# S5 outputs moved from the attention stretch into the scan stretch of a hybrid encoder layer

## The chip, the cores and the metric

The kernel runs as one program on one core of a Trainium2 chip. The metric is device time in microseconds (us); lower is better. Five engines work side by side, each on its own list of instructions: TensorE (PE, matmuls and transposes), VectorE (DVE), ScalarE (ACT), GpSimd (POOL) and SyncE (SP), which issues most DMAs. PSUM, the memory that TensorE writes, is shared out here in eight buffers.

## The reference, cut to what matters

One layer: a bidirectional S5 state space model with a GLU, beside a 4-head attention into 256 memory tokens; both outputs go through one projection, a layer norm, and a mixture of 16 experts. The part in question:

```python
bu = jnp.einsum('blgc,gpc->blgp', ug, b_bar)           # inputs of the states
_, states = lax.associative_scan(_ssm_combine, (a, bu), reverse=(direction == 1), axis=1)
y = y + jnp.real(jnp.einsum('gcp,blgp->blgc', cmat, states)).reshape(bsz, L, S5_WIDTH)
...
g = jax.nn.gelu(y)
return g * jax.nn.sigmoid(g @ w_glu + b_glu)
...
kv = (mem @ w_kv).reshape(bsz, mem.shape[1], 2, MEM_HEADS, MEM_HEAD_DIM)
s = jnp.einsum('blhd,bmhd->bhlm', q, kv[:, :, 0]) * (MEM_HEAD_DIM ** -0.5)
out = jnp.einsum('bhlm,bmhd->blhd', jax.nn.softmax(s, -1), kv[:, :, 1])
```

## The kernel before

There are 2048 tokens in 16 tiles of 128, and 32 S5 groups in 8 blocks of four. The sequence is cut into 128 chunks of 16 tokens: what happens inside a chunk is a matrix product, and only one state per chunk is scanned.

The first stretch projects the tokens (`inproj_u`) and builds the S5 matrices block by block (`s5_block`); these wait in DRAM (`wid` for a block's inputs, `wod` and `kd` for its outputs).

The scan stretch treats each block in three steps. `chunk_inputs` multiplies U by the loaded `wtl` on TensorE into a PSUM buffer `pvv`, and ScalarE copies it into the state `S`, two copies a block. `scan` then copies four pieces of a rotation table `R` out of `E` (ScalarE), rotates `S` (`turn_states`: one multiply of 128x1024 on VectorE, one on GpSimd, two adds on VectorE), runs eight recurrences on VectorE, rotates back (two multiplies again, one add on VectorE and one on GpSimd), and copies the result into `SS` with eight ScalarE copies. The blocks go 6, 7, 0, 1, ... 5. `R` has two buffers; the products `m` have one, and a spare part of `S` serves every other block. In the middle stands `kv`: the keys' and values' weights in four parts, each loaded, split into two halves of 16 bits (`kvh` on ScalarE, `kvl` on VectorE) and multiplied on TensorE, and at the end eight `kh` and eight `kl` copies on ScalarE.

The attention stretch interleaves two things in a fixed TensorE order. `s5_out` takes a block's four groups; a group is eight f32 matmul passes into `py`; two groups make one `gt` copy, and after every second block four times four transposes (`trg`) with a GELU follow (`gelu`: ScalarE square, VectorE, ScalarE tanh, VectorE), written into `gT`, which lies over `S`. `attention` goes through 16 tiles in three stages (scores and exponentials; transposed probabilities two tiles later; values three tiles later); `STEPS` says how many of these stages follow each piece of `s5_out`. The blocks 0 and 1 have no attention in between and run while the scan ends; from block 2 on two stages follow each piece. `glu_weights` loads the GLU's weights over `E` once the rotations have been read, and splits them (four ScalarE, four VectorE instructions). `glu` follows.

The order on the engines other than TensorE is set by a scheduler that places instructions by its own costs and keeps each engine's list fixed from then on. TensorE's order is as written inside `manual_schedule`.

Of the kernel before, what the change touches and what calls it, by code (L numbers as in the profile page):

```python
# [9 lines left out]
F32 = mybir.dt.float32  # L10
# [3 lines left out]
ALU = mybir.AluOpType  # L14
# [39 lines left out]
STEPS = (0,) * 8 + (1,) + (2,) * 39  # L54
ATL = (2, 3)
WIP = 3
# [16 lines left out]
class Kern:  # L73
# [97 lines left out]
    def front(self, fr):  # L171
# [17 lines left out]
        with ExitStack() as s5:  # L189
            up = s5.enter_context(self.pool("up", side="left"))  # L190
            self.U = up.tile([P, 2, G, P], F32, name="U")
            att = s5.enter_context(self.pool("att", side="left"))
            with ExitStack() as t0:
                self.inproj_u(t0, scp)
            ssp = s5.enter_context(self.pool("ssp", side="left"))
            self.SS = ssp.tile([P, 2, G, P + 2], F32, name="SS")
            self.nc.gpsimd.memset(self.SS[:, 0, :, 0:1], 0.0)
            self.nc.gpsimd.memset(self.SS[:, 1, :, P + 1:P + 2], 0.0)
            with ExitStack() as t2:
                self.ps1 = t2.enter_context(self.pool("ps1", bufs=3, space=PSUM))  # L200
                self.ps2 = t2.enter_context(self.pool("ps2", bufs=1, space=PSUM))
                order = list(range(NB - KEEP, NB)) + list(range(NB - KEEP))
                gtp = t2.enter_context(self.pool("gtp", bufs=GTB, side="left"))
                wp = [t2.enter_context(self.pool("wopa", bufs=2, side="left"))]
                with ExitStack() as t:
# [9 lines left out]
                gup = t2.enter_context(self.pool("gup", bufs=2, side="right"))  # L215
                wp.append(t2.enter_context(self.pool("wopb", bufs=2, side="right")))
                with self.tc.manual_schedule(engines={mybir.EngineType.PE}):
                    counts = iter(STEPS)
                    for b in range(NB):
                        if b == GELU:  # L220
                            self.glu_weights()
                        for _ in self.s5_out(b, gtp, wp, gup):
                            for _ in range(next(counts)):
                                next(steps, None)
                    for _ in steps:
                        pass
# [108 lines left out]
    def kv(self, att, t):  # L335
# [16 lines left out]
        for c2 in range(0, DC, 2):  # L352
            raw = kp.tile([P, 2, 512], F32, tag="raw", name=f"kraw{c2}")
            nc.sync.dma_start(raw, a["w_kv"][:, c2:c2 + 2])
            wh = kp.tile([P, 2, 512], F16, tag="kvh", bufs=1, name=f"kvh{c2}")
            wl = kp.tile([P, 2, 512], F16, tag="kvl", bufs=1, name=f"kvl{c2}")
            self.split_w(wh, wl, raw)
            for i in range(2):
                c = c2 + i
                ends = c == 0, c == DC - 1  # L360
                for k in range(2):
                    sl = slice(k * P, k * P + P)
                    self.mm3(kacc[k][:, :256], wh[:, i, sl], wl[:, i, sl], mh[:, c], ml[:, c], *ends)
                    self.mm3(vacc[k][:, :256], mh[:, c, sl], ml[:, c, sl], wh[:, i, 256:], wl[:, i, 256:], *ends)
# [321 lines left out]
    def turn_states(self, S, R, m, back):  # L686
        V, Q = self.nc.vector, self.nc.gpsimd
        tab = lambda i: R[:, i].unsqueeze(2).to_broadcast([P, GB // 2, 2, 2 * P])
        S, m = S.rearrange("p g h d k -> p g h (d k)"), m.rearrange("p a g h d k -> p a g h (d k)")
        V.tensor_tensor(m[:, 0], S, tab(0), op=ALU.mult)  # L690
        Q.tensor_tensor(m[:, 1], S[:, :, 1::-1], tab(1), op=ALU.mult)  # L691
        for h in range(2):
            op = ALU.add if h == back else ALU.subtract
            eng = Q if (back, h) in QADD else V
            eng.tensor_tensor(S[:, :, h], m[:, 0, :, h], m[:, 1, :, h], op=op)


    def scan(self, b):
# [4 lines left out]

        if b >= NB - KEEP or b % 2 == 0:
            m = self.scp.tile([P, 2, n, 2, 2, P], F32, tag="m", bufs=1, name=f"m{b}")
        else:
            m = self.spare.rearrange("p a g d k -> p (a g d k)").rearrange("p (a g h d k) -> p a g h d k", a=2, g=n, h=2, d=2)
# [71 lines left out]
    def s5_out(self, b, gp_, wp, gup):  # L779
# [6 lines left out]
        for gp in range(GB // 2):  # L786
            w = wp[b > 1 and gp]
# [50 lines left out]
    def glu(self):  # L838
        nc, a = self.nc, self.a
        V = nc.vector  # L840
        with ExitStack() as g:
# [6 lines left out]
            for t in range(4):  # L848
# [3 lines left out]
                for c in range(4):  # L852
# [3 lines left out]
                for o, c in [(o, c) for c in range(4) for o in range(4)] if t == 0 else [(o, c) for o in range(4) for c in range(4)]:  # L856
                    sl = slice(o * P, o * P + P)
                    self.mm3(po[o], wh[:, c, sl], wl[:, c, sl], gh[:, c], gl[:, c], c == 0, c == 3)
# [733 lines left out]
```

## Time and profile before

| what | value |
|---|---|
| median of 3 runs | 1091.31 us (1090.85 to 1091.59) |
| the profiled execution, its own time | 1091.53 us |
| its span, first to last instruction | 1089.7 us |
| mean granted TensorE clock | 0.931 |
| busy share of the span | PE 83%, DVE 76%, ACT 50%, POOL 49% |
| scan, first multiply to first attention exponential | 231.7 to 336.6 us |
| attention, to the first GLU matmul | 336.6 to 443.6 us |

The span is 1.8 us shorter than the execution, which has a fixed part outside the profile. The stretches of the last two rows are read from the timelines. Busy shares are means over stages with different limits, so each stretch is read by itself. The granted clock is a share of 2.4 GHz; TensorE has two levels, 1.2 and 2.4 GHz, and a mean between them says how long each held.

### The profile page before, as it was taken

How to read it: one execution, taken by the hardware profiler on the slowest of the kernel's cores; microseconds unless marked ns; L12 is line 12 of the kernel's file. 1: busy time of each engine (PE TensorE's matmuls, PEld its weight loads, DVE VectorE, ACT ScalarE, POOL GpSimd, SP SyncE). 2: the span in 40 equal slices, each digit the busy share in tenths (PEclk: the TensorE clock that was granted, in tenths of full speed). 3: DMA queues.
4: the chain of work that ended last, by engine and by line, in shares of the span. 5: the costliest groups of instructions: out<-in, count | busy, mean ns of one | idle time of the engine just before them, and what ended most of it. 6: DMA issues, size and time to landing. Idle time of an engine off the chain costs nothing. (4 is left out here: it accounts for less than half of the span.)

```text
span 1089.7 us, 18757 instructions
## 1 busy us (share of the span) xinstructions
PE 899.5 (83%) x7108; PEld 606.8 (56%) x7108; DVE 828.3 (76%) x1636; ACT 540.5 (50%) x1068; POOL 535.3 (49%) x379
## 2 busy tenths in 40 slices
PE   7777599985845999899999888698979987989880
PEld 4444465674734877444554447476657754755540
DVE  7999888969997666483585676467878787878774
ACT  5122243445748776477633312265656554746530
POOL 1475655426663331325945444525444566367454
PEclk9899799999887999999999987899999998999995
DMA  7113355275271422417736331476578669557531
GB/s 253 41 45 117 121 180 202 69 243 168 61 227 46 132 81 77 140 55 267 257 141 116 78 114 64 142 292 227 206 269 319 215 225 334 198 205 233 208 107 65
DMA packets 65199, 178.14 MB, mean 163 GB/s; under 512 B 15121, under 2 KB 33425, under 8 KB 57681
## 3 DMA queue, kind: packets, MB, share of 16 engines
q1 hardware_dynamic: 44800, 128.83, 36.2%
q0 software_dynamic: 20304, 48.07, 12.9%
q8 instruction: 57, 0.93, 0.3%
q14 instruction: 38, 0.30, 0.1%
HBM read 141.95 MB, written 58.49 MB: 184 GB/s over the span
## 5 line engine op out<-in xcount | busy, mean ns | idle before, releaser
L92 DVE SCALAR_TENSOR_TENSOR wl<-raw,wh 128x1024 f16<-128x1024 f32 x82 | 97.8, 1219 | 10.4 <-ACT wh L91 7.9
L91 ACT ACTIVATE wh<-raw 128x1024 f16<-128x1024 f32 x82 | 82.0, 1048 | 24.1 <-PE pg L109 13.8
L109 PE MATMUL pg<-xl,wh 128*128 128x288 f16 (+1 forms) x256 | 73.3, 288 | 3.0 <-DVE xl L1462 2.8
L110 PE MATMUL pg<-xh,wl 128*128 128x288 f16 (+1 forms) x256 | 73.3, 288 | 0.9 <-issue 0.9
L108 PE MATMUL pu<-xh,wh 128*128 128x288 f16 (+1 forms) x256 | 71.8, 283 | 2.4 <-DVE hl L1049 1.9
L108 PE MATMUL pg<-xh,wh 128*128 128x288 f16 (+1 forms) x256 | 73.5, 289 | 0.0
L1206 POOL DMA_INDIRECT xs<-xg,idxall x31 | 38.9, 1256 | 70.2 <-DVE xg L1499 40.9
L110 PE MATMUL pu<-xh,wl 128*128 128x288 f16 (+1 forms) x256 | 71.6, 282 | 1.5 <-issue 1.5
L109 PE MATMUL pu<-xl,wh 128*128 128x288 f16 (+1 forms) x256 | 71.6, 282 | 0.0
L109 PEld LDWEIGHTS <-wh 128*128 128x128 f16 x576 | 58.1, 101 | 19.0 <-issue 5.7
L108 PEld LDWEIGHTS <-wh 128*128 128x128 f16 x576 | 58.3, 101 | 18.5 <-issue 3.5
L110 PEld LDWEIGHTS <-wl 128*128 128x128 f16 x576 | 57.9, 101 | 17.5 <-issue 4.4
L108 PE MATMUL pq<-xh,S 128*128 128x128 f16 x256 | 51.0, 235 | 15.9 <-DVE OT L295 15.9
L743 POOL TENSOR_TENSOR pe<-pe,ri 128x1024 f32<-128x1024 f32 x16 | 30.3, 1895 | 55.5 <-DVE ri L742 38.8
L108 PE MATMUL pu<-winh,xh 128*128 128x512 f16 x128 | 49.7, 388 | 6.6 <-ACT winh L91 6.6
L1201 POOL DMA_INDIRECT xg<-x1d,idxall x31 | 37.9, 1222 | 32.9 <-DMA out_x<-xg,idxall 13.0
L108 PE MATMUL py<-wh,hh 128*128 128x512 f16 x120 | 45.9, 385 | 8.8 <-ACT hh L1048 4.6
L1462 DVE TENSOR_TENSOR xl<-pt,xh 128x512 f16<-128x512 f32 x60 | 39.5, 683 | 16.1 <-ACT xh L1461 10.1
L1461 ACT ACTIVATE xh<-pt 128x512 f16<-128x512 f32 x60 | 34.0, 592 | 35.8 <-PE pt L1458 29.5
L110 PE MATMUL pq<-xh,S 128*128 128x128 f16 x256 | 51.2, 235 | 0.4 <-DVE S L92 0.3
L1458 PE MATMUL pt<-ident,xg 128*128 128x128 f32 x240 | 37.8, 285 | 16.5 <-DVE xl L1462 7.6
L691 POOL TENSOR_TENSOR m<-S,R 128x1024 f32<-128x1024 f32 x10 | 30.4, 3045 | 42.0 <-DVE S L715 23.6
(471 smaller groups left out, 3163.6 us busy)
## 6 DMA issues: line engine op xcount, KB each, us to landing
raw<-in_w_gate SPq DMA_DIRECT2D x16, 1024.0 KB
raw<-in_w_up SPq DMA_DIRECT2D x16, 1024.0 KB
raw<-in_w_down SPq DMA_DIRECT2D x16, 1024.0 KB
xr<-in_xT SPq DMA_DIRECT2D x16, 512.0 KB
xs<-wo SPq DMA_DIRECT2D x16, 512.0 KB
wol<-xs SPq DMA_DIRECT2D x16, 512.0 KB
M<-kd SPq DMA_DIRECT2D x64, 128.0 KB
xres<-in_x SPq DMA_DIRECT2D x16, 512.0 KB
```

The source lines that it names most:

```text
L91: self.nc.scalar.activation(hi, raw, AF.Copy, scale=WS)
L92: self.nc.vector.scalar_tensor_tensor(lo, raw, WS, hi, op0=ALU.mult, op1=ALU.subtract)
L108: mm(ps, lh, rh, start=first, stop=False)
L109: mm(ps, lh, rl, start=False, stop=False)
L110: mm(ps, ll, rh, start=False, stop=last)
L691: Q.tensor_tensor(m[:, 1], S[:, :, 1::-1], tab(1), op=ALU.mult)
L743: nc.gpsimd.tensor_tensor(pe, pe, ri.unsqueeze(2).to_broadcast([P, 4, 256]), op=ALU.mult)
L1201: return self.nc.gpsimd.indirect_dma_start(out=out, out_offset=None, in_=src, in_offset=bass.IndirectOffsetOnAxis(ap=idx, axis=0))
L1206: st = self.nc.gpsimd.indirect_dma_start(out=self.xs, out_offset=bass.IndirectOffsetOnAxis(ap=si, axis=0), in_=z[:sz], in_offset=None, bou ...
L1458: nc.tensor.transpose(pt[:, i, off:off + sz], x[:sz, (d0 + i) * P:(d0 + i) * P + P], self.ident[:sz, :sz])
L1461: nc.scalar.activation(xh[:, ds_, :n], pt, AF.Copy)
L1462: nc.vector.tensor_tensor(xl[:, ds_, :n], pt, xh[:, ds_, :n], op=ALU.subtract)
```

## The change

The output of block n-2 is now issued in the turn of block n of the scan, so that the outputs of blocks 6, 7, 0, 1, 2 and 3 stand in the scan stretch, with the GELUs of blocks (6, 7), (0, 1) and (2, 3). `kv` becomes a generator and gives one of its four parts to each turn. Only blocks 4 and 5 stay with attention, five stages after each group, and all that is left before the last GELU. The spare part of `S` is no longer free, so every other block's products go into parts of `SS` (or, for block 5, into the input buffers, which are two instead of three). The GLU takes its four chunks in the order 3, 0, 1, 2. `glu_weights` is called before the last two outputs.

```diff
-STEPS = (0,) * 8 + (1,) + (2,) * 39
+PACE = 5
+REST = 99
-WIP = 3
+WIP = 2
...
                 with ExitStack() as t:
                     self.scp = t.enter_context(self.pool("scm", bufs=2, side="right"))
-                    for b in order[:KEEP]:
-                        self.scan(b)
-                    self.kv(att, t)
                     wip = t.enter_context(self.pool("wip", bufs=WIP, side="right"))
-                    for b in order[KEEP:]:
-                        self.chunk_inputs(b, [self.stored(b, q, wip) for q in range(GB // 2)], self.ps1, "s5")
-                        self.scan(b)
+                    inputs = lambda b: self.chunk_inputs(b, [self.stored(b, q, wip) for q in range(GB // 2)], self.ps1, "s5")
...
+                    for b in range(NB - KEEP, NB):
+                        self.scan(b, halves.get(b))
+                    inputs(0)
+                    keys = self.kv(att, t)
...
+                    for n in range(NB - KEEP):
+                        if n == 5:
+                            halves[n] = [wip.tile([P, 1024], F32, tag="wi", name=f"mw{i}") for i in range(2)]
+                        self.scan(n, halves.get(n))
+                        if n == 3:
+                            ends(slice(8, 24))
+                        next(keys, None)
+                        for k, _ in enumerate(out((n - KEEP) % NB)):
+                            if k == 0 and n + 1 < NB - KEEP:
+                                inputs(n + 1)
+                    for _ in keys:
+                        pass
                 steps = self.attention(t2)
+                self.glu_weights()
                 wp.append(t2.enter_context(self.pool("wopb", bufs=2, side="right")))
...
+                for n in range(NB - KEEP, NB):
+                    for k, _ in enumerate(out(n - KEEP)):
+                        for _ in range(REST if k == GB and n % 2 else PACE):
+                            next(steps, None)
...
             self.split_w(wh, wl, raw)
+            yield
...
-            w = wp[b > 1 and gp]
+            w = wp[gp % len(wp)]
...
-                for c in range(4):
+                for c in (3, 0, 1, 2):
```

The scheduler places the other engines' instructions anew. ScalarE, from block 2's last rotation to block 3's first; before (`pvv` numbers begin with the block, `R3` is block 3's table, `kh`, `kl` and `kth` are the keys' halves):

```order
L377 ACTIVATE kh_2837<-kth0_2977 64x256 x4
L641 ACTIVATE S_78<-pvv31_3237 128x512
L681 ACTIVATE R3_3255<-E_1328 128x4x65
L682 ACTIVATE R3_3255<-E_1328 128x4x63
L681 ACTIVATE R3_3255<-E_1328 128x4x65
L682 ACTIVATE R3_3255<-E_1328 128x4x63
L378 ACTIVATE kl_2838<-ktl0_2978 64x256 x4
L641 ACTIVATE S_78<-pvv40_3288 128x512
L370 ACTIVATE kth1_2991<-pk1_2852 128x256
L720 ACTIVATE SS_2756<-S_78 64x2x128 x8
```

and now (`gu3` is the GELU of blocks 6 and 7, the `SS` copies are block 2's):

```order
L701 ACTIVATE R4_3498<-E_1328 128x4x65
L845 ACTIVATE gu30_3152<-gu30_3152 128x512
L702 ACTIVATE R4_3498<-E_1328 128x4x63
L845 ACTIVATE gu31_3162<-gu31_3162 128x512
L739 ACTIVATE SS_2756<-S_78 64x2x128 x8
L843 ACTIVATE gu32_3172<-trg72_3167 128x512
L843 ACTIVATE gu33_3182<-trg73_3177 128x512
L845 ACTIVATE gu32_3172<-gu32_3172 128x512
L845 ACTIVATE gu33_3182<-gu33_3182 128x512
L93 ACTIVATE kvh4_3243<-kraw4_3241 128x1024
L661 ACTIVATE S_78<-pvv30_3260 128x512
L661 ACTIVATE S_78<-pvv31_3278 128x512
```

Block 3's two inputs stood ahead of block 1's and 2's `SS` copies before; now they stand behind R4, block 2's `SS` copies, a GELU and a key split. The same place between blocks 4 and 5 now reads on ScalarE:

```order
L845 ACTIVATE gu03_3492<-gu03_3492 128x512
L386 ACTIVATE vh_2917<-pv0_2931 128x256
L390 ACTIVATE kth0_3553<-pk0_2929 128x256
L386 ACTIVATE vh_2917<-pv1_2932 128x256
L397 ACTIVATE kh_2915<-kth0_3553 64x256 x4
L398 ACTIVATE kl_2916<-ktl0_3554 64x256 x4
L390 ACTIVATE kth1_3567<-pk1_2930 128x256
L661 ACTIVATE S_78<-pvv50_3592 128x512
L397 ACTIVATE kh_2915<-kth1_3567 64x256 x4
L398 ACTIVATE kl_2916<-ktl1_3568 64x256 x4
L661 ACTIVATE S_78<-pvv51_3610 128x512
```

Before, block 5's two input copies stood ahead of both `R4` and `R5`; now the second of them stands behind all the last key copies. VectorE between blocks 3 and 4 now reads:

```order
L710 TENSOR_TENSOR SS_2756<-S_78,R3_3322 128x1024
L715 TENSOR_TENSOR S_78<-SS_2756 128x2x256
L94 SCALAR_TENSOR_TENSOR kvl6_3380<-kraw6_3377,kvh6_3379 128x1024
L94 SCALAR_TENSOR_TENSOR E_1328<-E_1328 128x512 x4
L710 TENSOR_TENSOR m4_3497<-S_78,R4_3498 128x1024
```

The split of the GLU's weights (the rows on E), which stood among the attention tiles before, is now ahead of block 4's first multiply (the row with m4).

## Rows read from the trace of the kernel before

**Rows 1.** Windows: us, then busy us of PE, PEld, DVE, ACT, POOL, PEclk, DMA share, GB/s
```profile
260.00:280.00 20.00, 13.64 (x162) 11.26 (x162) 19.90 (x26) 9.11 (x23) 11.19 (x5) 0.83 0.27 88
320.00:340.00 20.00, 3.90 (x19) 3.07 (x18) 15.20 (x24) 11.61 (x32) 11.21 (x5) 0.59 0.38 109
336.60:443.60 107.00, 96.12 (x877) 80.63 (x877) 69.50 (x130) 77.83 (x226) 30.32 (x16) 0.96 0.30 92
```
**Rows 2.** Timeline of VectorE in the scan: start us, us, engine, line, op, tiles, count
```profile
231.79 3.38 DVE L690 TENSOR_TENSOR m<-S,R 128x1024 f32<-128x1024 f32 x1
235.28 1.29 DVE L695 TENSOR_TENSOR S<-m 128x512 f32<-128x512 f32 x2
...
251.26 2.62 DVE L715 TENSOR_TENSOR_SCAN S<-decay,S 128x128 f32<-128x128 f32 x8
253.91 1.23 DVE L690 TENSOR_TENSOR m<-S,R 128x1024 f32<-128x1024 f32 x1
...
330.10 0.68 DVE L825 SCALAR_TENSOR_TENSOR gu<-gu,trg 128x512 f32<-128x512 f32 x1
```
**Rows 3.** Timeline of GpSimd in the scan
```profile
231.66 2.43 POOL L691 TENSOR_TENSOR m<-S,R 128x1024 f32<-128x1024 f32 x1 [17.61 <-ACT S L641]
...
254.02 3.33 POOL L691 TENSOR_TENSOR m<-S,R 128x1024 f32<-128x1024 f32 x1 [4.97 <-DVE S L715]
...
279.95 3.85 POOL L691 TENSOR_TENSOR S<-S,R 128x1024 f32<-128x1024 f32 x1 [2.25 <-DVE S L715]
283.76 3.33 POOL L691 TENSOR_TENSOR m<-S,R 128x1024 f32<-128x1024 f32 x1
...
329.00 3.39 POOL L691 TENSOR_TENSOR S<-S,R 128x1024 f32<-128x1024 f32 x1 [3.77 <-DVE S L715]
332.47 1.77 POOL L695 TENSOR_TENSOR S<-S 128x512 f32<-128x512 f32 x1
```
**Rows 4.** Timeline of ScalarE in the scan
```profile
230.52 1.07 ACT L641 ACTIVATE S<-pvv 128x512 f32<-128x512 f32 x2
...
243.76 0.42 ACT L681 ACTIVATE R<-E 128x260 f32<-128x260 f32 x1 [3.17 <-POOL m L691]
...
245.01 1.04 ACT L91 ACTIVATE kvh<-kraw 128x1024 f16<-128x1024 f32 x1
245.95 3.40 ACT L720 ACTIVATE SS<-S 64x256 f32<-64x256 f32 x8
...
282.20 1.69 ACT L377 ACTIVATE kh<-kth 64x256 f16<-64x256 f16 x4
...
329.29 1.05 ACT L824 ACTIVATE gu<-trg 128x512 f32<-128x512 f32 x2
330.82 0.63 ACT L826 ACTIVATE gu<-gu 128x512 f32<-128x512 f32 x1 [0.47 <-DVE gu L825]
...
340.40 2.18 ACT L91 ACTIVATE E<-E 128x512 f16<-128x512 f32 x4
```
**Rows 5.** Timeline of ScalarE, attention: the first exponential, and two later tiles
```profile
336.64 0.47 ACT L740 ACTIVATE pe<-pS,nm 128x256 f32<-128x256 f32 x1
...
351.86 0.47 ACT L740 ACTIVATE pe<-pS,nm 128x256 f32<-128x256 f32 x1 [0.65 <-DVE nm L737]
...
353.67 0.39 ACT L776 ACTIVATE OT<-po 128x256 f16<-128x256 f32 x1
354.70 1.09 ACT L758 ACTIVATE th<-pT 128x512 f16<-128x512 f32 x2 [0.63 <-PE pT L757]
```
**Rows 6.** Timeline of TensorE, attention: two groups of outputs, and the first GLU matmul
```profile
348.68 0.60 PE L802 MATMUL py<-M,U 128*128 128x256 f32 x2
...
350.41 0.27 PE L734 MATMUL pS<-kh,OT 128*128 128x256 f16 x1
...
359.29 0.60 PE L802 MATMUL py<-M,U 128*128 128x256 f32 x2
...
443.56 0.39 PE L108 MATMUL pg<-gh,E 128*128 128x512 f16 x1
```

More of the change, by code (lines that the diff above doesn't have):

```diff
@@ L196, in front, with ends @@
             self.SS = ssp.tile([P, 2, G, P + 2], F32, name="SS")
-            self.nc.gpsimd.memset(self.SS[:, 0, :, 0:1], 0.0)
-            self.nc.gpsimd.memset(self.SS[:, 1, :, P + 1:P + 2], 0.0)
+            def ends(gs):
+                self.nc.gpsimd.memset(self.SS[:, 0, gs, 0:1], 0.0)
+                self.nc.gpsimd.memset(self.SS[:, 1, gs, P + 1:P + 2], 0.0)
+            ends(slice(0, 8))
+            ends(slice(24, G))
             with ExitStack() as t2:
@@ L201, in front @@
                 self.ps2 = t2.enter_context(self.pool("ps2", bufs=1, space=PSUM))
-                order = list(range(NB - KEEP, NB)) + list(range(NB - KEEP))
                 gtp = t2.enter_context(self.pool("gtp", bufs=GTB, side="left"))
                 wp = [t2.enter_context(self.pool("wopa", bufs=2, side="left"))]
+                gup = t2.enter_context(self.pool("gup", bufs=2, side="right"))
+                out = lambda b: self.s5_out(b, gtp, wp, gup)
+                t2.enter_context(self.tc.manual_schedule(engines={mybir.EngineType.PE}))
@@ new lines, in front @@
+                    late = [self.SS[:, d, 8:24].rearrange("p g k -> p (g k)") for d in range(2)]
+                    halves = {b: [late[d][:, o:o + 1024] for o in (0, 1024)] for b, d in ((NB - 1, 0), (0, 1), (1, 0))}
+                    halves[3] = [late[d][:, 1040:2064] for d in range(2)]
+                    for b in range(NB - KEEP, NB):
[12 more added lines that the diff above has]
+                                inputs(n + 1)
@@ L214, in front @@
+                    for _ in keys:
+                        pass
                 steps = self.attention(t2)
-                gup = t2.enter_context(self.pool("gup", bufs=2, side="right"))
+                self.glu_weights()
                 wp.append(t2.enter_context(self.pool("wopb", bufs=2, side="right")))
[L217 to L226, printed above, removed]
+                for n in range(NB - KEEP, NB):
+                    for k, _ in enumerate(out(n - KEEP)):
+                        for _ in range(REST if k == GB and n % 2 else PACE):
+                            next(steps, None)
@@ L688, in turn_states @@
         tab = lambda i: R[:, i].unsqueeze(2).to_broadcast([P, GB // 2, 2, 2 * P])
-        S, m = S.rearrange("p g h d k -> p g h (d k)"), m.rearrange("p a g h d k -> p a g h (d k)")
-        V.tensor_tensor(m[:, 0], S, tab(0), op=ALU.mult)
-        Q.tensor_tensor(m[:, 1], S[:, :, 1::-1], tab(1), op=ALU.mult)
+        S = S.rearrange("p g h d k -> p g h (d k)")
+        V.tensor_tensor(m[0], S, tab(0), op=ALU.mult)
+        Q.tensor_tensor(m[1], S[:, :, 1::-1], tab(1), op=ALU.mult)
         for h in range(2):
@@ L694, in turn_states, with scan @@
             eng = Q if (back, h) in QADD else V
-            eng.tensor_tensor(S[:, :, h], m[:, 0, :, h], m[:, 1, :, h], op=op)
-    def scan(self, b):
+            eng.tensor_tensor(S[:, :, h], m[0][:, :, h], m[1][:, :, h], op=op)
+    def scan(self, b, m=None):
         nc = self.nc
@@ L702, in scan @@
         S, SS = self.S[:, gs], self.SS
[L704 to L707, printed above, removed]
+        if m is None:
+            m = self.scp.tile([P, 2, 1024], F32, tag="m", bufs=1, name=f"m{b}")
+            m = [m[:, i] for i in range(2)]
+        m = [x.rearrange("p (g h k) -> p g h k", g=n, h=2) for x in m]
         R = self.rotations(b)
@@ L855, in glu @@
                 po = [ps.tile([P, 512], F32, tag="pg", name=f"pg{t}{o}") for o in range(4)]
-                for o, c in [(o, c) for c in range(4) for o in range(4)] if t == 0 else [(o, c) for o in range(4) for c in range(4)]:
+                co = (3, 0, 1, 2)
+                for o, c in [(o, c) for c in co for o in range(4)] if t == 0 else [(o, c) for o in range(4) for c in co]:
                     sl = slice(o * P, o * P + P)
-                    self.mm3(po[o], wh[:, c, sl], wl[:, c, sl], gh[:, c], gl[:, c], c == 0, c == 3)
+                    self.mm3(po[o], wh[:, c, sl], wl[:, c, sl], gh[:, c], gl[:, c], c == 3, c == 2)
                 for o in range(4):
```

## The prediction

> **What bounds the kernel now.** I read three things in this order: busy time by stretch [rows 1], the timelines of VectorE and GpSimd in the scan [rows 2, 3], and those of ScalarE and TensorE, which say when work is ready [rows 4 to 6]. The change acts between the scan's first multiply at 231.66 [rows 3] and the first GLU matmul at 443.56 [rows 6]; what follows is the same work, so I price these 212 us and let the rest move along.
>
> In the scan VectorE is full and TensorE is not (19.90 and 13.64 of 20 us in the first window [rows 1]). The reader is to see that VectorE and GpSimd take turns. A VectorE multiply takes 1.23 at 253.91; the same one, issued 0.13 after GpSimd's at 231.66, takes 3.38 and ends when both could have run one after the other. So a block costs the sum of both engines: a pair of multiplies 3.5 (231.66 to 235.17), two adds 1.3, eight recurrences 2.6, the second pair 3.4, together **10.8**, and 1.9 for the last adds [rows 2, 3]. Eight times 12.7 is 101.6; from 231.66 to the end of the last add at 334.24 there are 102.6. Nothing else holds the scan: block 2's first multiply starts at 283.76, when block 1's last ends (279.95 and 3.85) [rows 3]. Its inputs had been ready.
>
> In attention TensorE is busy 96.1 of 107 us [rows 1], so there its work is the price.
>
> **The change, part by part.** I take ends of last multiplies as marks: T1 for block 1 (283.80 now), T5 for block 5 (332.39 now: 329.00 and 3.39) [rows 3].
>
> *Up to T1.* Three of the four key splits on VectorE leave this part (the second and later ones come behind T1); the first now stands ahead of block 6's adds and waits for its load and ScalarE's half (1.04 [rows 4]). Less 3 times about 1.1, plus some 3 of waiting: nothing, with 2 us on either side. Products in other places and smaller memsets cost nothing: the same instructions.
>
> *T1 to T5.* Here lies the largest term. A block's first multiply on either engine needs both copies of its inputs, and ScalarE makes them where its list has them. Before, they were far ahead. Now each block from 2 on has them behind what the block before it has just finished, so the two busiest engines stand while ScalarE goes through its list. Prices from [rows 4]: four rotation copies 1.25 (243.76 to 245.01), eight SS copies 3.40, an input copy 0.53, a key split 1.04, two squares 1.05, a tanh 0.53 to 0.63, four kh or kl copies 1.69, four halves of the GLU's weights 2.18.
> - Block 2, behind T1: the last adds and a key split on the shared turn (some 2 to 3), eight SS copies 3.4, one input copy 0.5: **6.3**.
> - Block 3, behind block 2's last multiply, for whose table the rotation copies wait: 1.25, two tanh 1.05, SS 3.4, two squares 1.05, two tanh 1.05, key split 1.04, two inputs 1.07 make 9.9. VectorE's answer between square and tanh is 0.68 [rows 2]; with changes of engine I take **10.9**.
> - Block 4: rotation 1.25, SS 3.4, key split 1.04, input 0.53, GLU weights 2.18, input 0.53 make 8.9. The GLU's weights may be loaded only when the rotation copies have read E; no row shows that load alone, so I bound its extra wait by 0 and 4 and take 2: **10.9**. Its split on VectorE (four times 0.6) ends with it.
> - Block 5: 0.7 for the add, SS 3.4, two squares, two tanh 2.1, three small copies of values and keys 1.0, four groups of four key copies 6.76, one more small copy 0.35, two inputs 1.07: 15.4, taken as **15.5**.
>
> Between them lies each block's own 10.8. T5 comes 6.3 + 10.9 + 10.9 + 15.5 + 4 x 10.8 = 86.8 after T1; before it came 48.6 after. **The scan is 38 us longer.** The GELUs cost VectorE little by themselves: the one at 330.10 takes 0.68 while GpSimd multiplies [rows 2, 3].
>
> *T5 to the first exponential.* Before, 4.2 (336.64 [rows 5]). Now ScalarE has SS copies to 4.1, the last gt copy, then the GELU of blocks 2 and 3 with two pairs of squares and tanh and VectorE's answers between: 10.3. **6 us more.**
>
> *Attention.* From 348.68 to 359.29 TensorE does two tiles and three groups of S5 output without a pause; a group is 1.73 (348.68 to 350.41), so a tile is (10.61 - 5.19)/2 = 2.71 [rows 6]. Blocks 2 to 7 had 24 groups here, blocks 4 and 5 have 8. Of the rest 16 x 2.71 + 8 x 1.73 = 57.2. At the present ratio, 96.1 busy of 107 [rows 1], that is 63.6; subtracting 16 groups from 107, and 3.6 for 32 transposes, gives 75.7. With fewer groups between the tiles a pause for probabilities weighs more, and a last GELU must still end before the GLU; I take **71**. 36 us are saved.
>
> *Sum.* First exponential 336.6 + 38.2 + 6.0 = 380.9, GLU 71 later, 451.9 against 443.6: 8.3 more. The profiled execution took 1091.5, the median is 1091.3, so they can stand for each other: **1100**. The other order of the GLU's chunks I cost at nothing; its start waits for the last GELU either way, and TensorE is then the bound. Loads: each turn of over 20 us brings an output's four transfers, issued one turn ahead; were that cover gone, the wait would be theirs, on TensorE, which has slack in the scan.
>
> What the sum hangs on is that a ready input copy doesn't pass a waiting SS copy. In the row at 243.76 ScalarE stood 3.17 us for GpSimd's multiply, with the key split next on its list [rows 4]. The Trainium skill ("PSUM — Partial Sum Buffer", section "Engine vs sequencer instructions") says that ScalarE's, VectorE's and GpSimd's queues are strict first-in-first-out. The trace agrees in this one place. By that rule the 1100 holds; by an engine that picked what is ready, the inputs would come early and the second rival below would result.
>
> **The rivals.**
> 1. *Attention at ScalarE's pace (faster).* A tile costs ScalarE four exponentials 1.81 (351.86 to 353.67), 0.28 to 0.39, and two probabilities' copies 1.05 [rows 5]: 3.2. Sixteen are 51, four gt copies 2, start and last GELU 4: 57 instead of 71, and the kernel comes at 1086. It decides where the stage falls under 62.8 (107 less 44.2). For it speaks that TensorE's 57.2 fits; against it, that even TensorE's full stage has 11 us of pauses now. **0.18.**
> 2. *The scan stays at its bound (much faster).* The handovers hide, T5 is later only by the weights' split 2.4, attention starts 8 later and saves 36: 1064. The place is ScalarE's list between two blocks; the point, whether each block's first multiply starts within 2 us of the last adds. Against it speaks the written order, for it that ScalarE is only 46% busy in the first window [rows 1]. **0.08.**
> 3. *TensorE at 1.2 GHz in the scan (slower still).* At 320 to 340 the clock was 0.59 with TensorE busy 3.9, at 260 to 280 0.83 with 13.6 [rows 1]. After block 4 TensorE has eight groups to finish before the last GELU, 13.8 at 2.4 GHz, 27.7 at 1.2 GHz; starting some 14 behind block 4's last multiply they then end at 42, and the GELU needs them at 30: 12 later, and 5 more for block 3's inputs. 1117. TensorE will have more to do than in either window, so I hold this for less likely. **0.12.**
> 4. *Gain and loss cancel*, within 2 us: handovers 6 to 8 us shorter in all (no wait for the GLU's load, VectorE's answers hidden). **0.12.**
>
> **How the numbers follow.** My forecast, 1094 to 1108, has **0.50**. About 0.2% (2 us) is what a measurement of this kernel tells from no change. Faster holds rivals 1 and 2: 0.26; same is rival 4: 0.12; slower is the forecast and rival 3: 0.62. The range for 8 in 10 leaves out rival 2 and the outer part of rival 3: 1084 to 1115; it contains the ends of 63.6 and 75.7 for attention (1092 to 1105) and 2 us a handover on either side.
>
> **What would show it.** Right: in the new profile VectorE and GpSimd both idle for some 6, 9, 9 and 14 us ahead of the first multiplies of blocks 2, 3, 4 and 5, put down to ScalarE's input copies; block 5's last multiply near 371; first exponential near 381; the GLU near 452. The share of VectorE between 300 and 370 would fall below 15 of 20. Wrong: block 5's last multiply before 350 (rival 2); a tile every 3.2 to 3.4 us in attention (rival 1); a clock near 0.5 at 340 to 370 with transposes late (rival 3); or waits on DMA ahead of the output matmuls, which I priced at nothing.

## The result and the profile after

The changed kernel takes **1117.5 us** (median of 4 runs, 1113.9 to 1124.6) against 1091.1 of the kernel before in the same session: ratio **1.0244**, 95% interval 1.0209 to 1.0278. The prediction was 1100 with a range to 1115: the sign was right, the size was not. The profiled execution took 1118.1 with a span of 1116.3, 26.6 more than the span before.

Four marks divide those 26.6. "After the GLU" is from its first matmul to the end of the span.

| mark | before | predicted | after |
|---|---|---|---|
| end of block 5's last multiply | 332.4 | 371 | 370.0 |
| first exponential | 336.6 | 380.9 | 381.1 |
| first GLU matmul | 443.6 | 452 | 465.6 |
| from there to the end | 646.1 | 646.1 | 650.7 |

So the marks of the scan came out within a microsecond (in part by luck, see below), attention was 13.5 us longer than forecast (84.5, not 71), and 4.6 us more lie behind the GLU, where nothing was priced.

The scan first. GpSimd's timeline of the changed kernel, the first and last multiplies around the handovers (the columns are those of [rows 3]):

```profile
277.11 3.32 POOL L711 TENSOR_TENSOR SS<-S,R 128x1024 f32<-128x1024 f32 x1 [4.44 <-DVE S L734]
286.64 3.39 POOL L711 TENSOR_TENSOR m<-S,R 128x1024 f32<-128x1024 f32 x1 [4.01 <-ACT S L661]
294.05 3.32 POOL L711 TENSOR_TENSOR m<-S,R 128x1024 f32<-128x1024 f32 x1 [4.01 <-DVE S L734]
...
310.17 3.45 POOL L711 TENSOR_TENSOR SS<-S,R 128x1024 f32<-128x1024 f32 x1 [10.95 <-ACT S L661]
317.63 3.38 POOL L711 TENSOR_TENSOR SS<-S,R 128x1024 f32<-128x1024 f32 x1 [4.01 <-DVE S L734]
...
331.86 2.63 POOL L711 TENSOR_TENSOR m<-S,R 128x1024 f32<-128x1024 f32 x1 [8.75 <-ACT S L661]
339.65 3.33 POOL L711 TENSOR_TENSOR m<-S,R 128x1024 f32<-128x1024 f32 x1 [5.17 <-DVE S L734]
359.30 3.39 POOL L711 TENSOR_TENSOR mw<-S,R 128x1024 f32<-128x1024 f32 x1 [14.47 <-ACT S L661]
366.70 3.32 POOL L711 TENSOR_TENSOR mw<-S,R 128x1024 f32<-128x1024 f32 x1 [4.01 <-DVE S L734]
```

The first multiplies of blocks 2, 3, 4 and 5 now wait for ScalarE's input copies (L661). From the end of one block's last multiply to the next block's first, the handovers are 6.2, 12.8, 10.9 and 16.3 us; before, block 2's multiply began as block 1's ended [rows 3]. What ScalarE does ahead of block 5's first multiply, and then the first exponential, from its timeline:

```profile
343.80 2.15 ACT L739 ACTIVATE SS<-S 64x256 f32<-64x256 f32 x5 [1.17 <-DVE S L715]
...
350.88 1.68 ACT L397 ACTIVATE kh<-kth 64x256 f16<-64x256 f16 x4
352.59 1.69 ACT L398 ACTIVATE kl<-ktl 64x256 f16<-64x256 f16 x4
354.31 0.38 ACT L390 ACTIVATE kth<-pk 128x256 f16<-128x256 f32 x1
354.59 0.59 ACT L661 ACTIVATE S<-pvv 128x512 f32<-128x512 f32 x1
355.20 1.69 ACT L397 ACTIVATE kh<-kth 64x256 f16<-64x256 f16 x4
356.91 1.69 ACT L398 ACTIVATE kl<-ktl 64x256 f16<-64x256 f16 x4
358.63 0.60 ACT L661 ACTIVATE S<-pvv 128x512 f32<-128x512 f32 x1
...
381.08 0.47 ACT L759 ACTIVATE pe<-pS,nm 128x256 f32<-128x256 f32 x1
```

It works nearly without a pause from 343.8 to 359.2, and the second input copy stands behind eight copies of keys that follow the first. TensorE's timeline shows that this copy's matmuls had ended at 353.9 (350.23 and 3.71), 4.7 us before. ScalarE's order is not the whole of it: these matmuls themselves began only at 350.2, behind the fourth group of transposes of a GELU, for which TensorE had waited 10.1 us until 344.45, and behind the last key matmuls. Block 3's inputs were late in the same way: their matmuls ran from 305.73 to 309.44, and ScalarE stood 0.85 and 1.15 us for them. TensorE's timeline also has the last of the eight groups of blocks 2 and 3, and the end of attention:

```profile
350.23 3.71 PE L658 MATMUL pvv<-U,wtl 128*64 128x128 f32 x64
...
372.49 0.59 PE L824 MATMUL py<-wol,SS 128*128 128x256 f32 x2
...
457.91 1.53 PE L835 MATMUL trg<-ident,gt 128*128 128x128 f32 x12
461.45 0.63 PE L835 MATMUL trg<-ident,gt 128*128 128x128 f32 x4 [2.01 <-DVE S L846]
465.61 1.87 PE L110 MATMUL pg<-gh,E 128*128 128x512 f16 x4 [3.54 <-ACT gh L872]
467.27 0.63 PE L111 MATMUL pg<-gl,E 128*128 128x512 f16 x1
```

The last values end at 457.9. The last four groups of transposes, their GELU and ScalarE's first copies for the GLU follow with nothing beside them: 7.7 us. Windows of the changed kernel (columns as in [rows 1]): the stretch ahead of block 5, and the tiles of attention from the first exponential to the last values.

```profile
340.00:360.00 20.00, 15.55 (x120) 13.12 (x121) 8.72 (x15) 16.41 (x37) 5.45 (x3) 0.75 0.07 19
381.00:457.90 76.90, 62.28 (x692) 49.61 (x690) 49.18 (x97) 55.13 (x180) 30.28 (x16) 0.98 0.13 42
```

Among the tiles TensorE is busy 62.3 of 76.9 us, ScalarE 55.1; before, TensorE was busy 96.1 of 107 over the whole stretch [rows 1]. No engine is full. What TensorE waits for from 381 to 466 (waited for, us in total, times, longest):

```profile
PE po L792 <- DVE tl L778: 8.9, 13, 0.9
PE pg L110 <- ACT gh L872: 3.5, 1, 3.5
PE po L792 <- ACT th L777: 2.4, 4, 0.8
PE trg L835 <- DVE S L846: 2.0, 1, 2.0
```

### The profile page after: what moved, and what is told of

Read it like the earlier page. It is cut to its first block, busy times and chain, and to the rows that moved or that the text cites. A ratio compares the mean times of both kernels' runs of the same rounds, so it can differ in the third digit from the quotient of the medians.

```text
span 1116.3 us, 18810 instructions
## 1 busy us (share of the span) xinstructions
PE 904.5 (81%) x7108; PEld 607.5 (54%) x7108; DVE 823.6 (74%) x1636; ACT 541.3 (48%) x1068; POOL 536.7 (48%) x383
## 5 line engine op out<-in xcount | busy, mean ns | idle before, releaser
L111 PEld LDWEIGHTS <-wh 128*128 128x128 f16 x576 | 57.7, 100 | 15.5 <-issue 2.5
L110 PE MATMUL pq<-xh,S 128*128 128x128 f16 x256 | 49.8, 232 | 17.9 <-DVE OT L314 17.9
L1519 DVE SCALAR_TENSOR_TENSOR xg<-py,idxall,xg 128x512 f32<-128x512 f32 x60 | 43.2, 743 | 24.0 <-DMA xg<-xs,idxall 19.4
L111 PE MATMUL pu<-winl,xh 128*128 128x512 f16 x128 | 49.7, 388 | 0.2 <-DVE winl L94 0.2
L112 PE MATMUL pq<-xh,S 128*128 128x128 f16 x256 | 49.8, 232 | 0.0
L111 PE MATMUL pq<-xl,S 128*128 128x128 f16 x256 | 49.6, 231 | 0.0
L112 PE MATMUL pu<-winh,xl 128*128 128x512 f16 x128 | 49.4, 386 | 0.0
```

Source lines behind the costliest of these rows:

```text
L110: mm(ps, lh, rh, start=first, stop=False)
L111: mm(ps, lh, rl, start=False, stop=False)
L112: mm(ps, ll, rh, start=False, stop=last)
L1519: nc.vector.scalar_tensor_tensor(xg[:sz, hs], py[:sz], gate, xg[:sz, hs], op0=ALU.mult, op1=ALU.add, **acc)
```

## The experiments

Twelve kernels ran. The median of the kernel before moved between sessions (1085.8 to 1091.4), so kernels are compared by their ratio to it. The other columns are read from each run's one profile, in us; attention, whose code is the same in the changed kernel, ahead and kvearly, took 84.5 to 85.6 in these three, so differences of several us in it are no scatter; "block 5" is the end of its last multiply.

| run | median | ratio to before (95%) | block 5 | first exp. | GLU | attention |
|---|---|---|---|---|---|---|
| changed kernel | 1117.5 | 1.0244 (1.0209 to 1.0278) | 370.0 | 381.1 | 465.6 | 84.5 |
| ahead | 1116.5 | 1.0253 (1.0177 to 1.0328) | 350.5 | 385.2 | 470.8 | 85.6 |
| kvearly | 1122.7 | 1.0323 (1.0261 to 1.0384) | 378.9 | 391.5 | 476.3 | 84.8 |
| lag4 | 1111.5 | 1.0198 (1.0111 to 1.0285) | 371.1 | 383.2 | 461.5 | 78.3 |
| tail | 1106.3 | 1.0171 (1.0111 to 1.0231) | 370.6 | 382.7 | 461.0 | 78.3 |
| lag35 | 1112.5 | 1.0172 (1.0109 to 1.0235) | 370.4 | 382.5 | 458.3 | 75.8 |
| plain | 1124.7 | 1.0279 (1.0215 to 1.0344) | 369.5 | 396.5 | 474.5 | 78.0 |
| tail_lag35 | 1100.0 | 1.0138 (1.0099 to 1.0177) | 369.8 | 381.4 | 453.8 | 72.4 |
| late2 | 1105.4 | 1.0113 (1.0048 to 1.0177) | 337.5 | 372.8 | 453.6 | 80.8 |
| before_lag35 | 1092.4 | 1.0001 (0.9972 to 1.0029) | 331.0 | 335.2 | 443.0 | 107.8 |
| spread | 1090.7 | 1.0053 (1.0029 to 1.0076) | 331.4 | 335.6 | 441.7 | 106.1 |
| spread_lag35 | 1084.4 | 0.9979 (0.9954 to 1.0005) | 330.3 | 334.5 | 439.2 | 104.7 |
| two | 1124.3 | 1.0334 (1.0303 to 1.0365) | 350.3 | 380.4 | 482.0 | 101.6 |

**The handovers.** Run ahead: the inputs two blocks ahead.

```diff
 inputs(0)
+inputs(1)
...
-if k == 0 and n + 1 < NB - KEEP:
-    inputs(n + 1)
+if k == 0 and n + 2 < NB - KEEP:
+    inputs(n + 2)
```

> The changed kernel, but a block's inputs are computed two blocks ahead instead of one, so that ScalarE has both input copies on its list ahead of the SS copies of the block before. Theory (handovers): the first multiplies of blocks 2, 3, 4 and 5 stand because those copies come late. Then the waits of 6.2, 12.7, 10.9 and 16.3 us between a block's last multiply and the next one's first fall to some 2, 6, 6 and 6, the last multiply of block 5 ends near 344 instead of 370, and the kernel comes at about 1092. What stays is the GELU's answers and the GLU's weights on VectorE. Rival (the outputs' loads or TensorE's order hold the blocks): the last multiply of block 5 stays at 362 to 372 with the waits put down to something else, and the kernel at 1110 to 1118.

Block 2's first multiply no longer waits for block 1: it runs ahead of block 1's last one (276.05 and 280.86 below). The handovers into blocks 3, 4 and 5 are 5.9, 12.0 and 6.5, and block 5 was done 19.5 us earlier, at 350.5 where 344 was expected. So the theory holds for blocks 2, 3 and 5. Into block 4 nothing was gained: its input matmuls ran only from 318.10 to 321.81, behind the wait that follows here. And the kernel gained nothing: the first exponential came 4 us later. TensorE's waits up to 385 in this run, GpSimd in the scan and at its end, and the first exponential on ScalarE:

```profile
PE trg L836 <- DVE S L847: 19.9, 3, 9.8
PE py L822 <- ACT S L662: 14.4, 4, 11.2
PE pvv L659 <- DMA wtl<-wid: 13.7, 4, 10.7
```
```profile
276.05 2.49 POOL L712 TENSOR_TENSOR m<-S,R 128x1024 f32<-128x1024 f32 x1 [1.17 <-ACT S L662]
280.86 5.78 POOL L712 TENSOR_TENSOR SS<-S,R 128x1024 f32<-128x1024 f32 x1 [2.31 <-DVE S L735]
...
339.79 3.39 POOL L712 TENSOR_TENSOR mw<-S,R 128x1024 f32<-128x1024 f32 x1 [4.66 <-ACT S L662]
347.19 3.31 POOL L712 TENSOR_TENSOR mw<-S,R 128x1024 f32<-128x1024 f32 x1 [4.01 <-DVE S L735]
```
```profile
385.20 0.47 ACT L760 ACTIVATE pe<-pS,nm 128x256 f32<-128x256 f32 x1 [0.47 <-DVE nm L757]
```

There is a second chain, through TensorE's list, that is as long. The fourth group of transposes of an output needs a buffer that the GELU gives back, the GELU's VectorE operations stand behind the scan's, and the last key matmuls, eight groups and four groups of transposes stand behind that wait on TensorE's list. It is there in the changed kernel too: its eight groups end at 373.1 (372.49 and 0.59), within 1.2 us of the SS copies on ScalarE (370.84 to 374.25). Taking one chain away left the other. The two are not independent: this wait ended at 344.5 in the changed kernel, behind block 4's scan, and at 355.0 here, behind block 5's: the scheduler had placed the GELU's VectorE operations elsewhere.

Run kvearly: the keys and values at once, as before.

```diff
-keys = self.kv(att, t)
+keys = iter(list(self.kv(att, t)))
```

> The changed kernel, but the four parts of the keys' and values' matmuls run one after the other behind block 7's scan instead of one in each turn. Theory (handovers): ScalarE's copies of keys and values (8.1 us of its list) leave the stretch ahead of block 5's first multiply, whose wait falls from 16.3 to about 8; blocks 2 to 4 lose a key split each (1.0); up to the end of block 1 some 2 to 4 us are added. The kernel gains 5 to 10 us: 1108 to 1113. Rival (the GELU's answers fill that stretch anyway): block 5's wait stays over 13 and the time within 3 us of the changed kernel's 1117.

The handovers became 3.5, 10.7, 5.9 and 12.7, together 13 us shorter: with the keys' work moved away they do shorten, though block 5's 12.7 is nearer to the rival's 13 than to the 8 of the theory. The cost ahead of block 1, which I had put at 2 to 4, was 21.6 (its last multiply ends at 302.0, not 280.4), and the kernel came out slower. GpSimd's timeline has the wait:

```profile
291.26 3.39 POOL L711 TENSOR_TENSOR SS<-S,R 128x1024 f32<-128x1024 f32 x1 [19.25 <-ACT S L661]
```

In TensorE's written order block 1's inputs then stand behind all of the keys. Without the four parts this order loses more than it gains.

**Attention.** Run plain: the eight groups ahead of the tiles instead of between them.

```diff
-for _ in range(REST if k == GB and n % 2 else PACE):
+for _ in range(99 if k == GB and n % 2 else 0):
```

> The changed kernel, with the eight groups of the last two S5 outputs ahead of attention instead of between its tiles; the same work, no group between two tiles. Theory (loop): a bare tile takes 3.6 to 3.8 us from transpose to transpose, TensorE idle for about 1 of them; the groups cost 14 to 18 ahead of the tiles instead of 1.73 each between them, and the kernel stays within 4 us of 1117 or is a little slower. Rival (the prediction's own: a tile costs TensorE's 2.71, and what pauses there are come from the groups and their copies): a bare tile takes 2.7 to 3.2, its sixteen 44 to 51, and the kernel gains 5 to 12 us.

This is the measurement of a bare tile that the trace before did not hold. TensorE's timeline, from one tile's transposes to the next, and the window over nine such tiles:

```profile
414.82 1.09 PE L776 MATMUL pT<-ident,pe 128*128 128x128 f32 x8
...
416.72 0.25 PE L792 MATMUL po<-th,vh 128*64 128x128 f16 x2
...
418.15 0.25 PE L792 MATMUL po<-tl,vh 128*64 128x128 f16 x2 [0.67 <-DVE tl L778]
...
418.55 1.09 PE L776 MATMUL pT<-ident,pe 128*128 128x128 f32 x8
...
423.08 1.09 PE L776 MATMUL pT<-ident,pe 128*128 128x128 f32 x8
```
```profile
414.82:451.59 36.77, 27.88 (x363) 21.89 (x360) 27.31 (x54) 29.63 (x96) 17.05 (x9) 1.00 0.01 2
```

A bare tile takes 3.7 and 4.5 us in turn, 4.09 on the mean (36.77 by nine), at the full clock and with no engine full (ScalarE, the busiest, 29.6 of 36.8). It is neither the 2.71 of the prediction nor the flat 3.7 of the expectation. The reason is the order: the transposes of a tile (pT) are followed by one tile's scores, and then by the values (po) of the tile just transposed, which need ScalarE's high and VectorE's low halves of it. TensorE stands for them once or twice per tile, and one engine's answer sends off the next. The kernel was 0.35% slower than the changed one by the ratios, within their intervals, and 7 us slower in the profile (1123.1 against 1116.3): 15.4 us later at the first exponential, 6.5 given back behind it. One of the eight groups runs ahead of the first exponential in the changed kernel too; so the seven between the tiles (12.1 us) had hidden about half of themselves in those waits.

Runs lag4 and lag35: the values one step later, then the transposes one and the values two steps later, with buffers for it.

```diff
-ATL = (2, 3)
+ATL = (2, 4)     # lag35: (3, 5), and bufs=4 for "pe"
...
-tag="th", name
+tag="th", bufs=3, name
-tag="tl", name
+tag="tl", bufs=3, name
```

> The changed kernel, but in attention the values of a tile are taken four steps behind its scores instead of three, with three buffers for the probabilities' two halves. Theory (a loop over three engines): a tile takes 3.7 us where no S5 output lies between (transposes at 451.01 and 454.79, and at 439.09 and 442.76), more than TensorE's 2.71 and ScalarE's 3.2, because TensorE's list has the values right behind the transposes of the same tile and stands for ScalarE's and VectorE's answers. One step more takes that wait away: a tile nears ScalarE's 3.2 or less, the time from the first exponential to the last values falls from 76.8 to 58 to 66, and the kernel gains 10 to 18 us: 1099 to 1107. Rival (ScalarE, VectorE or the clock sets the pace): the 76.8 stays within 3 us, and the kernel within 3 us of 1117.

> The changed kernel, with the transposes three steps behind a tile's scores and its values five behind (before: two and three), with one buffer more for the exponentials and for each half of the probabilities. With the values one step later TensorE no longer waited for the probabilities' low halves, but 6.2 us for GpSimd's product ahead of the transposes. Theory (loops over the engines set the tile, one behind the other): with both a step further off the tile nears ScalarE's 3.2 us with the groups beside it, the first exponential to the last values takes 58 to 66 instead of 76.8, and the kernel comes at 1098 to 1107. Rival (VectorE's reductions or ScalarE's order hold it, which this does not touch): 69 to 74 as with the values alone moved, and the kernel at 1108 to 1113.

From the first exponential to the GLU lag4 took 6.2 us less and lag35 8.7 less. To the last values it was 70.6 and 68.2 us, from 76.9, where 58 to 66 was expected; the kernels were 0.5 and 0.7% nearer to the one before, with intervals that overlap the changed kernel's, and lag35's 1112.5 is in its rival's range. The wait for the low halves (8.9 us in the changed kernel) was gone in lag4, but another took its place, for GpSimd's product ahead of the transposes:

```profile
PE pT L776 <- POOL pe L762: 6.2, 6, 2.4
```

In lag35 that is down to nothing, and TensorE waits 7.0 us for the exponentials that free the scores' buffer. Lags and buffers were changed together; buffers alone were not run. The transposes of all tiles, first and last start, tell the pace: before, changed kernel, plain, lag35 (one row of each; the columns are line, engine, operation, tiles, count, ns least/median/most, first and last start).

```profile
L757 PE MATMUL pT<-ident,pe x128: 272/273/476, 340.9 to 421.7; 128*128 128x128 f32 x128
```
```profile
L776 PE MATMUL pT<-ident,pe x128: 272/273/329, 385.6 to 455.6; 128*128 128x128 f32 x128
```
```profile
L776 PE MATMUL pT<-ident,pe x128: 272/273/476, 401.1 to 464.5; 128*128 128x128 f32 x128
```
```profile
L776 PE MATMUL pT<-ident,pe x128: 272/273/329, 390.3 to 448.4; 128*128 128x128 f32 x128
```

With 0.8 taken off for the last tile's own eight, fifteen tiles take 80.0, 69.2, 62.6 and 57.3 us. Not all groups lie among them; counted on TensorE's timelines and priced as in the prediction (2.71 a tile, 1.73 a group, and 2.7 for the 24 transposes of outputs among the tiles of the kernel before), this is what a tile takes and what is left as a pause:

| | before | changed | plain | lag35 |
|---|---|---|---|---|
| groups among the fifteen tiles | 16 | 7 | 0 | 6 |
| a tile, measured | 5.3 | 4.6 | 4.2 | 3.8 |
| a tile, by the prices | 4.7 | 3.5 | 2.7 | 3.4 |
| pause left | 0.6 | 1.1 | 1.5 | 0.4 |

(In lag35 one tile's scores and one tile's values fewer fall among the fifteen, which makes its pause look some 0.1 smaller.) The fewer groups, the longer the pause; with longer lags most of it goes, not all.

Run tail: the last transposes and the GELU between the tiles.

```diff
-PACE = 5
-REST = 99
+PACE = 4
+REST = 4
...
+for _ in steps:
+    pass
```

> The changed kernel, but the last four groups of transposes and their GELU stand between the tiles of attention (four steps after each of the twelve pieces, the rest of the steps behind) instead of behind the last tile. Theory: from the last values at 457.9 to the first GLU matmul at 465.6 TensorE does 2 us of transposes and waits for the GELU, then for ScalarE's copies for the GLU, which nothing covers; woven in, 5 to 7 of these 7.7 us go and 1 to 2 come back as transposes between the tiles. The first GLU matmul comes 4 to 6 us earlier, the kernel at 1111 to 1113. Rival (the GLU waits for something else, its first copies or the splits of the output weights on ScalarE): the gap stays over 5 us and the time within 2 us of 1117.

TensorE's and ScalarE's timelines at the end of attention:

```profile
459.74 0.25 PE L794 MATMUL po<-th,vl 128*64 128x128 f16 x2
460.98 1.02 PE L110 MATMUL pg<-gh,E 128*128 128x512 f16 x4 [0.99 <-ACT gh L874]
461.84 0.38 PE L111 MATMUL pg<-gl,E 128*128 128x512 f16 x1
```
```profile
460.03 0.38 ACT L797 ACTIVATE OT<-po 128x256 f16<-128x256 f32 x1 [1.40 <-PE po L794]
460.31 4.25 ACT L874 ACTIVATE gh<-S 128x512 f16<-128x512 f32 x8
```

The 7.7 us are 1.0, and the GLU starts 4.6 earlier, as expected. It also runs from its first matmul at 0.38 us each, where the changed kernel's first ones take 0.63, and is 1.7 shorter (41.6 against 43.3 to the first output matmul). The rest of the 9.6 us by which the span shrank lies in the later stages, of which more below.

Run tail_lag35, both together:

> The changed kernel with two edits together that were run apart: the last transposes and GELU between the tiles, and transposes three, values five steps behind the scores. Theory (the attention term was missed by two separate costs, the loop over the engines and the uncovered tail): the first GLU matmul comes earlier by the sum of what each gave, 4.6 and 7.3 us: near 453.7 instead of 465.6, which is the place the prediction gave it (452), and the kernel near 1105 (1101 to 1107). Rival (both edits win the same idle time): the first GLU matmul at 457 to 461, the kernel at 1107 to 1112.

The first GLU matmul came at 453.8, where 453.7 was expected and the prediction had 452:

```profile
453.81 1.02 PE L110 MATMUL pg<-gh,E 128*128 128x512 f16 x4 [0.99 <-ACT gh L874]
```

Attention took 72.4 us, and the ratio is 1.0138; applied to the 1091.3 of the prediction that is 1106, inside the 1101 to 1107 expected (the median itself, 1100.0, belongs to the session in which the kernel before took 1085.8). The two costs add up at the first GLU matmul (4.6 and 7.3 us apart, 11.8 together), and with both gone the attention term of the prediction (71) is nearly met. The kernel is still slower than the one before, by 1.0 to 1.8%.

**Versions that should have been faster.** Run late2 put four outputs in the scan and the other four among the tiles, with the inputs two blocks ahead and the lags and the tail mended.

```diff
-for k, _ in enumerate(out((n - KEEP) % NB)):
-    if k == 0 and n + 1 < NB - KEEP:
-        inputs(n + 1)
+if n + 2 < NB - KEEP:
+    inputs(n + 2)
+if n >= 2:
+    for _ in out((n - 4) % NB):
+        pass
...
-for n in range(NB - KEEP, NB):
+for n in range(4, NB):
```

> A version meant to keep what the change gains without what it loses: the inputs two blocks ahead; the outputs of only four blocks (6, 7, 0, 1) in the scan, four turns behind it; the outputs of blocks 2 to 5 between the tiles of attention, two steps after each piece, the rest of the steps behind; transposes three and values five steps behind the scores. Theory (handovers on ScalarE and a TensorE list that holds attention back behind the outputs): block 5's last multiply ends near 342 instead of 370, the first exponential comes near 354 instead of 381, attention takes TensorE's 16 x 2.71 and 16 x 1.73 with some pauses, 74 to 80, the GLU starts near 432 (before: 443.6), and the kernel comes at 1074 to 1088, under both kernels or level with the one before. Rival (something else holds the first exponential, as in the run with the inputs ahead, where it came at 385 though block 5 was done at 350): first exponential after 372, kernel over 1100.

Block 5 ended at 337.5, only 5 us later than before, so the groups of two outputs hardly cost the scan anything; most of their GELU ran behind it (ScalarE's part until 346.0). The first exponential came at 372.8 all the same, and the rival held: TensorE stood up to 9.5 us for the GELU and had the last keys and the eight groups of blocks 0 and 1 left when the scan was done. Its waits from 300 to 372:

```profile
PE trg L840 <- DVE S L851: 11.5, 2, 9.5
PE py L826 <- ACT S L666: 9.5, 1, 9.5
```

Run two kept the order of the kernel before and only put two more outputs' matmuls, without GELU, ahead of attention, with a second output tile paid for by input buffers (WIP 1 instead of 3, GTB 2 instead of 1).

```diff
-GTB = 1
-WIP = 3
+GTB = 2
+WIP = 1
...
-for b in range(NB):
-    for _ in self.s5_out(b, gtp, wp, gup):
+for b, part in ((6, 0), (7, 0), (0, 0), (1, 0), (7, 1), (1, 1), (2, 0), (3, 0), (3, 1), (4, 0), (5, 0), (5, 1)):
+    for _ in self.s5_out(b, gtp, wp, gup, part):
```

> The kernel before, with four outputs' matmuls (blocks 6, 7, 0, 1) in the shade of the scan instead of two, and their transposes and GELU still in attention: two buffers for the outputs' tile, paid for with one input buffer instead of three; scan, inputs and keys stand as before. Theory (the outputs cost nothing in the scan as long as their GELU and the inputs' copies do not come between two blocks): the scan ends within 5 us of the 334.2 of before, the first exponential near 337 to 344, attention with 16 groups and 12 transposes takes 95 to 100 instead of 107, and the kernel comes at 1080 to 1090. Rival (one input buffer is too few: each block's inputs wait for a load and its matmuls): the scan ends 10 to 40 us later, the kernel at 1095 to 1125.

The rival held. (This run also has the GLU's chunks in the order of the changed kernel.) TensorE's waits up to 380:

```profile
PE pvv L641 <- DMA wtl<-wid: 38.3, 10, 9.0
```

The scan ended 18 us later, and the outputs came late as well. Four outputs with the input buffers left alone were not tried: a second output tile takes 8 KB of a partition, as much as two input buffers.

Three runs changed attention in the kernel before: the longer lags by lag35's edit (before_lag35), the steps between the pieces (spread, below), and both (spread_lag35).

```diff
-STEPS = (0,) * 8 + (1,) + (2,) * 39
+STEPS = (0,) * 8 + (2, 1) * 20
```

> The kernel before, with the transposes three and the values five steps behind the scores (two and three now) and the same buffers more as in the changed kernel's run. Theory: there 24 groups of S5 output fill most of TensorE's waits, its 96.1 busy of 107 leave 4 to 8 us to be had; attention ends with TensorE nearly full and the kernel gains 3 to 8 us: 1080 to 1086. Rival (TensorE is the bound there and the pauses are at its ends): within 2 us of 1088 to 1091.

> The kernel before, with only the numbers of attention's steps between the pieces of S5 output changed: two and one in turn instead of two, so that all 24 groups stand between the tiles and none behind the last (now eight, 13.9 us). Theory (a group between tiles costs about half its time as long as the tiles wait for each other): from the first exponential to the first GLU matmul 98 to 103 us instead of 107, the kernel gains 4 to 9 us: 1082 to 1087. Rival (TensorE's 96.1 us of work is the bound already and the pauses stand at the ends): within 2 us of 1091.

> The kernel before with the steps two and one in turn, and with the transposes three, the values five steps behind the scores. Theory: with all groups between the tiles and the loops over the engines loosened TensorE is full: 96 to 101 us instead of 107, the kernel 1080 to 1085, a little below the run with the steps alone. Rival: the loops don't count where groups fill the waits; the same time as with the steps alone, within 2 us.

In none was attention as short as expected; the steps alone were even 0.5% slower, and where that went the profile doesn't show. Attention took 107.8, 106.1 and 104.7 us against 107. With 24 groups to fill its waits TensorE has little left to win there, and what was won between tiles came back in part at the end: ahead of the first GLU matmul TensorE stood 3.1 us for the last GELU in before_lag35 and 7.1 in spread_lag35. The median of the third, 1084.4, lies in the range expected only because the kernel before took 1085.8 in that session. It is 0.7% faster than the second, with intervals that don't overlap, of which the stretch of attention shows 1.5 us; so the longer lags are worth something in this kernel too once the steps are spread, for a reason that stays open. The last of the three is level with the kernel before (0.9979, interval 0.9954 to 1.0005); no run beat both kernels by more than its uncertainty.

## Why the prediction was wrong in size

- **What bounds the scan, and the handovers (6.3, 10.9, 10.9, 15.5): right in size**, measured 6.2, 12.8, 10.9, 16.3, with block 5 done at 370.0 for 371, **and in part in mechanism.** Run ahead shows that the input copies hold the blocks: issued earlier, 20 us go. VectorE's 12.0 and 8.7 of 20 us from 320 to 360 are the sign that was named. But the prediction saw only ScalarE's list. For block 3 ScalarE stood 2.0 us for the input matmuls, which is the 1.9 that this handover is too long; for block 5 those matmuls ended 11.0 us after block 4's last multiply, and only the last 4.7 before the copy are ScalarE's order alone.
- **Block 5 to the first exponential, 10.3: right in number** (11.1), but here too the prediction saw only ScalarE's side. TensorE's list ended at about the same time in the changed kernel, and in ahead, with the scan 20 us shorter, it kept the first exponential at 385. The delay of the first exponential had two chains of about equal length, not one.
- **Up to block 1: nothing, with 2 either side; measured 3.4 earlier** (280.4 for 283.8), outside by 1.4, and given back in the handovers, which are 2.6 longer in sum than forecast. That block 5's end came out so close is luck to this extent.
- **The attention term, "I take 71": this is the step that failed.** It was 84.5. The prediction took TensorE's work per tile (2.71 and 1.73 a group), read where groups filled every pause [rows 6]. It did say that a pause would weigh more with fewer groups, and still went below the 75.7 that leaves the pauses as they were. In fact they grow, from 0.6 to 1.1 us a tile. The steps of a tile wait for each other across three engines; a bare tile takes 4.1 us, in which TensorE is busy 3.1 (the same work back to back took 2.71), and the groups had been the filling. The bound that I thought too high, 75.7, was still too low: it took every group of the 16 for its full 1.73. The measured balance is 10.8 us among the tiles (87.7 to 76.9) for nine groups fewer (16 to 7; the first of the eight now runs ahead of the first exponential) and 32 transposes, worth 19.2 of TensorE; and 11.6 behind the last tile (19.2 to 7.6), where eight groups, 13.9 us, had stood alone before, less a tail that is longer than before. Together 22.4, not 36.
- **"A last GELU must still end before the GLU" was named and not priced.** It is 7.7 us with the copies behind it. Together with the loop it is nearly the whole miss of this term: with it woven in and the loop loosened the run comes to 72.4. That this is near the 71 is partly chance: the 71 was a choice between 63.6 and 75.7, not a price of these two things.
- **What follows the GLU: "let the rest move along".** It was 4.6 us longer. Over the profiles here, all with the same work behind the GLU but for the order of its chunks, this stretch takes from 641.0 to 652.7 us (two and spread_lag35), the kernel before among them at 646.1 and, with nothing but its lags changed, at 650.2. So 4.6 is within what this stretch scatters, and no cause in the change is shown. It should have been in the range.
- **The rivals.** Rival 1 (ScalarE's 3.2 a tile) and rival 2 did not come. Rival 3 named the very time, 1117, for a reason that hardly occurred: the groups from 353 to 373 ran at 0.59 us a pair, the price of [rows 6] at the full clock (0.70 after a wait); only the key matmuls ahead of them, from 345.3 to 349.8, took 0.42 us each and not the 0.27 of those behind them. Rival 4 did not come. The last sign named, waits on DMA ahead of the output matmuls, came small: 3.7 us from the scan's start to the first exponential, against 2.3 before.

## What to carry to other kernels

Work that fills an engine's waits is worth only what it takes beyond those waits: before taking it away, look for the loop underneath (which instruction waits for whose answer to which earlier one), and price the bare iteration by that loop, not by the busiest engine. Where a chain of handovers is found, ask what the next engine's list would end at if it were gone; here it ended at the same time. And what stands behind the last iteration with nothing beside it is paid in full: it is the cheapest thing to weave in.

## What was not expected

A tile's time alternates, 3.7 and 4.5 us, in a steady state with next to no load in flight (2 GB/s; 418.55, 423.08 and so on above). And a group of S5 output between tiles cost 0.9 us on the mean where it takes 1.73 alone ((69.2 - 62.6) by 7, changed kernel against plain). That mean hides two kinds: from one tile's transposes to the next, four tiles with a group took 4.4 to 4.5 us, no longer than every second bare one, while the other three took 5.5, 6.9 and 8.4 (from 385.59, 407.42 and 430.68). Why these three differ stays open.
